# A streaming encoder layer on one core: three blocks of rows with eight products in place of the seven of the Strassen scheme

## Chip, core and metric

The kernel runs on one core of a Trainium2 chip. The metric is the device time of one execution in microseconds (us). The engines are TensorE (PE, with its weight loads as PEld), VectorE (DVE), ScalarE (ACT), GpSimd (POOL) and SyncE (SP, which here only issues transfers). Each works through its own queue in order.

## What is computed

One layer for 4096 prompt rows and 32 sample rows of width 1024. The rows are normalised, go through one input projection and two groups of heads, and the two halves go through an output projection:

```python
h = rms_norm(x, g_pre) * (1 + scale[:, None]) + shift[:, None]
proj = h @ w_in
z, xbc, dt_raw, u, v, gt = jnp.split(proj, [i1, i2, i3, i4, i5], axis=-1)
xbc, conv_new = causal_conv(xbc, conv_prev, conv_w, conv_b)
...
y, ssm_new = ssd_scan(xs, dt, a, bm, cm, ssm_prev)      # scan over chunks of 64 rows
ssd_out = (y + d_skip * xs) * jax.nn.silu(z)
v_n = layer_norm(v, g_v, beta_v)
gmlp_out = jax.nn.silu(gt) * u * gmlp_spatial(v_n, w_s, b_s)
mix = jnp.concatenate([ssd_out, gmlp_out], axis=-1) @ w_out
out = x + gate[:, None] * rms_norm(mix, g_post)
```

All of it is float32. `w_in` is 1024 x 5648, `w_out` 2048 x 1024.

## The kernel before

Weights and rows are split into a high and a low float16 half, and each product is the sum of three float16 matmuls (`PARTS`). The prompt is worked in eight blocks of 512 rows; the sample rows run along with block 3. A block goes: `super_step(0)` (B and C of the scan), the products for dt, the output projection of the block before it (16 weight tiles), `v_stage` (v, 14 tiles), and `super_step(1)` to `super_step(8)`. Each of the nine steps makes two pairs of 128-column strips, x and z, or gate and u. Work between them (conv, scan, spatial gating, row preparation of the next block) is put off with `later(lag, fn)` and called at a `tick` in a step, and a scheduler then lays out each engine's queue.

A step is a 2 x 2 block product with the seven products of the Strassen scheme in Winograd's form. `STEPS` lists them, each with 256 of the rows' columns: 7 x 2 x 12 = 168 matmuls. Sums of rows are made once a block in `phase_a_split` (L254 on VectorE, slots 4 to 6 of the rows' region); regions R0 and R1 alternate between blocks. Sums of weights are made once, in block 0: `stage_load` brings four strips of `w_in` (`stg`), `stage_squares` (L327, ScalarE) and `stage_scale` find a power of two for each and scale it (L341 on VectorE, or on ScalarE), and `wtile` makes a tile of each product:

```python
src = operand(s, w0[:, 0:512], w0[:, 512:1024], w1[:, 0:512], w1[:, 512:1024], ...)   # sums on VectorE, L302 to L308
split(wt[:, pi, 0], wt[:, pi, 1], src, nc.gpsimd if pi else nc.vector)                 # hi: ScalarE L266, lo: L267
nc.gpsimd.dma_start(out=w_dram[k][s], in_=...)                                         # L357, kept for the later blocks
```

`v_tile` does the same for v (tiles `wm`, sums `vtmp`, strips `vw`). Later blocks read the tiles back over SP's queue (L347 for `wt<-wd`, L409 for `wm<-vd`). Four slots hold weight tiles, and `wfetch(4)` asks for tiles up to four ahead. Results leave PSUM through `leave` (`LEAVES`): L661 on ScalarE where a quarter begins, L659 on VectorE where a product is added to it.

In block 1 the tiles of the output projection are made too: `o_tile` loads `wf`, and `split_w` makes hi (L295) and lo (L296) on VectorE.

Of the kernel before, what the change touches and what calls it, by code (L numbers as in the profile page):

```python
# [18 lines left out]
P = 128  # L19
# [34 lines left out]
PARTS = ((0, 0), (0, 1), (1, 0))  # L54

# [15 lines left out]
def hybrid_step_kernel(ctx: ExitStack, tc: tile.TileContext, io: dict, out: list):  # L71
# [143 lines left out]
    def new_rows(st, b):  # L215

        if st is prompt:
            st.hN = region(b, "hTp")
        else:
            st.hN = wk.tile([P, 3, 2, 4, st.T], F16, tag="hTs", name="hTs", bufs=1)  # L220
# [15 lines left out]
    def phase_a_split(st, ps, u, q, alt=False):  # L236
# [24 lines left out]
        for i, (src, slots, cs) in enumerate(parts):  # L261
            split(hN[:, slots, 0, q, cs], hN[:, slots, 1, q, cs], src, nc.vector if alt and i else nc.gpsimd)
# [17 lines left out]
    w_dram = [[dram.tile([P, 2048], F16, name=f"wd{k}_{s}", tag=f"wd{k}_{s}") for s in range(7)] for k in range(NSS)]  # L280
    v_dram = [dram.tile([P, 2048], F16, name=f"vd{j}", tag=f"vd{j}") for j in range(14)]
# [16 lines left out]
    def operand(s, a11, a12, a21, a22, tmp):  # L298

        tt = nc.vector.tensor_tensor  # L300
        if s == 1:
            tt(tmp, a21, a22, op=ALU.add)  # L302
        elif s == 2:
            tt(tmp, tmp, a11, op=ALU.subtract)
        elif s == 4:
            tt(a21, a11, a21, op=ALU.subtract)
        elif s == 5:
            tt(tmp, a12, tmp, op=ALU.subtract)  # L308
        return (a11, tmp, tmp, a12, a21, tmp, a22)[s]

# [3 lines left out]
    def stage_load(k):  # L314

        w = stage[k] = Work()
        w.f = [slots[(4 * k + n) % 8] for n in range(4)]
        for pi, (kind, i) in enumerate(SUPER[k]):
            for j in range(2):
                off = OFFS[kind][j] + i * P  # L320
                nc.sync.dma_start(out=w.f[2 * pi + j].rearrange("p (k c) -> p k c", c=P), in_=w_in_v[:, :, off:off + P])

    def stage_squares(k):
        w = stage[k]
        w.ss = small([P, 4], "wsq")
        for n in range(4):
            nc.scalar.activation(tmp2(prompt, "junk").bitcast(BF16), w.f[n], AF.Square, accum_out=w.ss[:, n:n + 1])  # L327

    def stage_scale(k):
        w = stage[k]  # L330
        s, inv = small([P, 4], "wsc"), scw[:, 4 * k:4 * k + 4]
        pow2_of_ssq(ssq_total(w.ss), [P, 4], "wp4", s, inv)
# [4 lines left out]
        for n in range(4):  # L337
            if n % 2:
                nc.scalar.activation(w.f[n], w.f[n], AF.Identity, scale=s[:, n:n + 1])
            else:  # L340
                nc.vector.tensor_scalar(w.f[n], w.f[n], s[:, n:n + 1], None, op0=ALU.mult)  # L341

    def wtile(k, s, first):
# [5 lines left out]
        w = stage[k]  # L349
        if s == 1:  # L350
            w.tmp = big("wtmp")
# [6 lines left out]
        return wt  # L358

# [32 lines left out]
    def mtile(d, idx, parts, s, first):  # L392
# [10 lines left out]
    vtmp = []  # L403

    def v_tile(s, h, first):
# [5 lines left out]
        if not vscale[0].known:  # L411
            for half in range(2):
                vscale[half].total()
                nc.vector.tensor_mul(sc_v[:, half:half + 1], vscale[half].inv, a_inv)
        if s == 0:
            for k in (2 * h, 2 * h + 1, 2 * h + 4, 2 * h + 5):
                nc.scalar.activation(vw[0][k], vw[0][k], AF.Identity, scale=vscale[0].s)
                nc.vector.tensor_scalar(vw[1][k], vw[1][k], vscale[1].s, None, op0=ALU.mult)
        if s == 1 and not vtmp:
            vtmp.extend(wk.tile([P, 512], F32, tag=tag, name="vtmp", bufs=n) for tag, n in (("xdtp", 1), ("xsTp", 3), ("xsTp", 3), ("xsTp", 3)))  # L420
        for qq in range(2):
            q = 2 * h + qq
            src = operand(s, vw[0][q], vw[0][q + 4], vw[1][q], vw[1][q + 4],
                          vtmp[2 * h + qq] if s else None)
            split(wt[:, qq, 0], wt[:, qq, 1], src, nc.gpsimd if qq else nc.vector)
# [15 lines left out]
    def plan():  # L441
# [6 lines left out]
        for b in range(NB):  # L448
            first = b == 0
            order.extend((wtile, (0, s, first)) for s in range(7))  # L450
            if b > 0:
                out(b == 1, 16)
            order.extend((v_tile, (s if first else STEPS_V[s][3], h, first)) for s in range(7) for h in range(2))
            order.extend((wtile, (k, s, first)) for k in range(1, NSS) for s in range(7))
# [210 lines left out]

    def super_step(k, active):
# [59 lines left out]
    def dt_rows_of(st, c):  # L726
# [115 lines left out]
    def by_rows(ps, x, w, first, last):  # L842
# [29 lines left out]
    def v_stage(active, first):  # L872
# [691 lines left out]
```

## Time and profile before

| | |
|---|---|
| median of 3 runs | 3115.49 us (3107.41 to 3121.79) |
| profiled execution, its time | 3119.56 us |
| profiled execution, span of the core | 3117.8 us |
| busy in the span | PE 2818.6, PEld 2016.7, DVE 1831.1, ACT 1499.6, POOL 1230.6 us |
| mean granted TensorE clock | 0.959 |
| DMA | 565.99 MB, 182 GB/s |

The span is the time from the first to the last instruction of the core, of one execution. A busy share over the whole span mixes block 0, in which weights are made, with blocks that only read them. The stretches used below are 0 to 104 us (opening and step 0 of block 0), 104 to 514 (the rest of block 0), 514 to 670 (block 1 to the end of its output projection), 670 to 893 (v and steps 1 to 8 of block 1) and 893 to 1240 (the same cycle of block 2 as a whole). The granted clock is the share of full speed (2.4 GHz) that TensorE was allowed; 0.5 is its lower level of 1.2 GHz.

### The profile page before, as it was taken

Reading aid. Unit: us, or ns where it says so; the run is one execution under the profiler, and the core shown is the slowest. Engines: PE = TensorE matmul, PEld = TensorE weight load, DVE = VectorE, ACT = ScalarE, POOL = GpSimd, SP = SyncE. Lnnn points to the kernel's source line nnn. Section 1 sums busy time; section 2 is a strip of 40 time slices with the busy share of each in tenths; the row PEclk is TensorE's granted clock in tenths of the full one; section 3 lists DMA queues with packets and bytes.
Section 4 is the critical chain, followed back from the end, with each engine's and each line's share of the span. In section 5 each row is a group of like instructions: output and inputs, shape, how many; then the busy total and the mean of one; then the engine's idle time right before and its main releaser. Section 6 shows DMA issues by size and latency. Waiting matters only on the chain. (4 is left out here: it accounts for less than half of the span.)

```text
span 3117.8 us, 56775 instructions
## 1 busy us (share of the span) xinstructions
PE 2818.6 (90%) x22010; PEld 2016.7 (65%) x22010; DVE 1831.1 (59%) x3938; ACT 1499.6 (48%) x3308; POOL 1230.6 (39%) x1143
## 2 busy tenths in 40 slices
PE   6766675789999999998999999999999999999988
PEld 2455564338874688546885478845885488747863
DVE  5987887956564554726557355545547455625562
ACT  4776764424544354534555335444545355424531
POOL 3556664323532254223553235432553144303441
PEclk7888888999999999999999999999999999999999
DMA  7655534566663766345564466636664566546652
GB/s 254 215 176 200 196 139 153 177 223 205 203 198 100 237 203 214 114 170 170 178 190 135 140 214 200 211 97 238 202 207 137 192 191 201 194 163 197 203 164 61
DMA packets 231335, 565.99 MB, mean 182 GB/s; under 512 B 26266, under 2 KB 76674, under 8 KB 231064
## 3 DMA queue, kind: packets, MB, share of 16 engines
q1 hardware_dynamic: 211400, 495.09, 49.9%
q0 software_dynamic: 19664, 67.27, 5.7%
q8 instruction: 172, 2.82, 0.4%
q14 instruction: 99, 0.81, 0.1%
HBM read 494.06 MB, written 68.20 MB: 180 GB/s over the span
## 5 line engine op out<-in xcount | busy, mean ns | idle before, releaser
L683 PE MATMUL ps_proj<-hTp,wt 128*128 128x256 f16 x12096 | 1428.4, 277 | 54.5 <-DVE zs L659 14.0
L683 PEld LDWEIGHTS <-wt 128*128 128x128 f16 x12096 | 1195.8, 100 | 226.9 <-issue 51.2
L851 PE MATMUL ps_out<-wm,mix 128*128 128x512 f16 x2880 | 654.0, 384 | 34.1 <-DVE wm L295 17.6
L851 PEld LDWEIGHTS <-mix 128*128 128x128 f16 x2880 | 281.7, 99 | 367.5 <-issue 39.5
L888 PE MATMUL ps_v<-wm,hTp 128*128 128x512 f16 x1344 | 306.9, 387 | 30.3 <-DMA wm<-vd 23.3
L888 PEld LDWEIGHTS <-hTp 128*128 128x128 f16 x1344 | 133.0, 100 | 197.0 <-issue 44.1
L1005 ACT ACTIVATE L<-L,acp 128x128 f32<-128x128 f32 x512 | 165.8, 390 | 144.8 <-DMA L<-acdp 132.3
L970 ACT ACTIVATE sq<-mix 128x512 f32<-128x512 f32 (+1 forms) x135 | 77.9, 582 | 306.8 <-POOL mix L1096 254.8
L723 DVE SCALAR_TENSOR_TENSOR xsT<-xp,cols,xsT 128x512 f32<-128x512 f32 (+1 forms) x216 | 223.0, 1035 | 3.7
L1068 DVE SCALAR_TENSOR_TENSOR hc<-hc,dcp,ps_s 128x64 f32<-128x64 f32 x384 | 79.9, 274 | 229.2 <-PE ps_s L1046 229.0
L1095 POOL TENSOR_TENSOR mix<-mix,E 128x512 f32<-128x512 f32 x72 | 84.1, 1167 | 305.5 <-DVE E L1091 296.7
L1016 POOL TENSOR_TENSOR L<-L,cb 128x512 f32<-128x512 f32 (+1 forms) x144 | 168.0, 1175 | 92.7 <-ACT L L1010 86.5
L267 POOL TENSOR_TENSOR mix<-ms,mix 128x512 f16<-128x512 f32 (+1 forms) x72 | 92.7, 1290 | 240.4 <-ACT mix L266 240.4
L974 POOL TENSOR_TENSOR acc<-acc,sq 128x512 f32<-128x512 f32 (+1 forms) x126 | 146.0, 1161 | 40.6 <-ACT sq L970 40.2
L267 POOL TENSOR_TENSOR hTp<-ta,hTp 128x512 f16<-128x512 f32 x64 | 78.1, 1221 | 199.4 <-ACT hTp L266 199.4
L267 POOL TENSOR_TENSOR v<-vt,v 128x512 f16<-128x512 f32 (+1 forms) x66 | 83.2, 1290 | 183.0 <-ACT v L266 183.0
L1102 POOL TENSOR_TENSOR mix<-mix,us 128x512 f32<-128x512 f32 x64 | 84.0, 1312 | 154.3 <-ACT us L661 142.7
L1038 POOL TENSOR_TENSOR xde<-xdt,dep 128x512 f32<-128x512 f32 x64 | 68.3, 1067 | 157.1 <-DVE xdt L1038 157.1
L254 DVE TENSOR_TENSOR tb<-ta 128x128 f32<-128x128 f32 x64 | 24.1, 376 | 171.2 <-ACT ta L245 166.2
L266 ACT ACTIVATE mix<-ms 128x512 f16<-128x512 f32 (+1 forms) x144 | 82.6, 582 | 83.1 <-DVE ms L1160 81.8
L1160 DVE TENSOR_TENSOR ms<-mix,sb 128x512 f32<-128x512 f32 (+1 forms) x144 | 108.5, 768 | 13.4 <-POOL hTp L267 8.9
L245 ACT ACTIVATE ta<-ps_xT,scol,gcol 128x256 f32<-128x256 f32 (+1 forms) x128 | 62.9, 543 | 104.4 <-PE ps_xT L232 90.3
(385 smaller groups left out, 4357.4 us busy)
## 6 DMA issues: line engine op xcount, KB each, us to landing
wt<-wd SPq DMA_DIRECT2D x441, 512.0 KB, 3.8
wm<-od SPq DMA_DIRECT2D x104, 512.0 KB, 3.5
wm<-vd SPq DMA_DIRECT2D x98, 512.0 KB, 5.1
L<-acdp SPq DMA_DIRECT2D x128, 256.0 KB, 4.4
wd<-wt POOLq DMA_DIRECT2D x63, 512.0 KB, 3.7
stg<-in_w_in_dram SPq DMA_DIRECT2D x36, 512.0 KB, 5.2
xa<-in_x_prompt_dram SPq DMA_DIRECT2D x32, 512.0 KB, 6.7
E<-acdp SPq DMA_DIRECT2D x128, 128.0 KB, 4.6
```

Of the source, the lines that this page charges most:

```text
L266: nc.scalar.activation(hi, src, AF.Copy)
L267: eng.tensor_tensor(lo, src, hi, op=ALU.subtract)
L683: nc.tensor.matmul(ps, wt[:, pi, a, q * P:(q + 1) * P], prompt.h[:, slot, b, q, :], start=(starts and h == 0 and n == 0), stop=(n == 11), ...
L723: nc.vector.scalar_tensor_tensor(dst, xp[:, k:k + Ts], w(k), dst, op0=ALU.mult, op1=ALU.add)
L851: nc.tensor.matmul(ps[c], x[kk][:, a, c * P:(c + 1) * P], w[:, kk, b, :], start=(first and n == 0), stop=(last and n == 5))
L888: nc.tensor.matmul(ps, prompt.h[:, slot, a, q, i * P:(i + 1) * P], wt[q // 2][:, q % 2, b, :], start=(starts and n == 0), stop=(n == 11), ...
L974: eng.tensor_tensor(st.accb if last else st.acc, st.acc, sq, op=ALU.add)
L1005: nc.scalar.activation(L[:, c, :], L[:, c, :], AF.Relu, scale=-1.0, bias=st.ac[:, c, 2 * j + hh:2 * j + hh + 1])
L1016: nc.gpsimd.tensor_tensor(w.L[hh], w.L[hh], st.cb[j // 4][0:st.Q], op=ALU.mult)
L1095: nc.gpsimd.tensor_tensor(w.m, w.m, w.E, op=ALU.add)
L1102: nc.gpsimd.tensor_tensor(m, m, w.d[1], op=ALU.mult)
L1160: nc.vector.tensor_tensor(t, m, sb, op=ALU.mult)
```

## The change

Blocks 0 to 2 (`b < FROM`) use `plain_step` and `v_plain`: eight products of 512 rows' columns, 96 matmuls a step and 192 for v, with the four plain tiles `PLAIN`, and results that leave PSUM 512 wide on ScalarE. Their rows fill only slots 0 to 3. The tiles of weight sums (`SUMS`), which blocks 3 to 7 need, are made by 22 jobs in the unused slots 4 to 6 of the rows' region (`spare`): ten are called in block 1, twelve in block 2. A job loads two pieces of 512 KB, scales them, makes four sums, splits each and stores four pieces of 256 KB. Beside that `o_tile` makes hi on ScalarE, staged strips are loaded and squared in halves two steps ahead, the last of them in spare room, and the preparation of block 1's rows is called in step 7 in place of step 8.

```diff
+FROM = 3
+PLAIN = (0, 3, 7, 6)
+SUMS = (1, 4, 2, 5)
...
+        elif st.plN:
+            parts = [(t.rearrange("p (i t) -> p i t", i=4), slice(0, 4), slice(u * P, (u + 1) * P))]
...
+    def spare(rows):
+
+        return rows[:, 4:7].rearrange("p i a k t -> p (i a k t)").bitcast(F32)
...
-        for n in range(4):
-            if n % 2:
-                nc.scalar.activation(w.f[n], w.f[n], AF.Identity, scale=s[:, n:n + 1])
-            else:
-                nc.vector.tensor_scalar(w.f[n], w.f[n], s[:, n:n + 1], None, op0=ALU.mult)
...
         for pi in range(2):
-            w0, w1 = w.f[2 * pi:2 * pi + 2]
-            src = operand(s, w0[:, 0:512], w0[:, 512:1024], w1[:, 0:512], w1[:, 512:1024],
-                          w.tmp[:, pi * 512:(pi + 1) * 512] if s else None)
-            split(wt[:, pi, 0], wt[:, pi, 1], src, nc.gpsimd if pi else nc.vector)
+            n = 2 * pi + j
+            scaled_split(wt[:, pi, 0], wt[:, pi, 1], stage[k].f[n][kh], sw[:, 4 * k + n:4 * k + n + 1], pi)
...
+    def scaled_split(hi, lo, wf, s, way):
+
+        if way == 0:
+            split_w(hi, lo, wf, s)
+        else:
+            nc.vector.tensor_scalar(wf, wf, s, None, op0=ALU.mult)
+            split(hi, lo, wf, nc.gpsimd)
...
+    def sums_load(kind, k, i):
+
+        w = Work()
+        f = spare(prompt.h)
+        w.a, w.b, w.t, w.o = f[:, 0:1024], f[:, 1024:2048], f[:, 2048:2560], f[:, 2560:3072]
...
+                nc.sync.dma_start(out=dst.rearrange("p (k c) -> p k c", c=P), in_=w_in_v[:, :, off:off + P])
...
+        later(5, sums_scale, w)
+
+    def sums_scale(w):
+        nc.scalar.activation(w.a, w.a, AF.Identity, scale=w.s[0])
+        nc.vector.tensor_scalar(w.b, w.b, w.s[1], None, op0=ALU.mult)
+        later(1, sums_first, w)
+
+    def sums_first(w):
+        a11, a21, a22 = w.a[:, 0:512], w.b[:, 0:512], w.b[:, 512:1024]
+        nc.vector.tensor_tensor(w.t, a21, a22, op=ALU.add)
+        nc.vector.tensor_tensor(a21, a11, a21, op=ALU.subtract)
+        later(1, sums_split, w, 1, w.t, w.o)
+        later(2, sums_split, w, 4, a21, a22)
+        later(2, sums_second, w, a11, a21)
...
+    def sums_split(w, s, src, out):
+
+        o = out.bitcast(F16)
+        split(o[:, 0:512], o[:, 512:1024], src, nc.gpsimd)
+        nc.gpsimd.dma_start(out=w.dst[s], in_=o)
...
         for hi, lo, wf in parts(wt):
-            split_w(hi, lo, wf, s)
+            nc.scalar.activation(hi, wf, AF.Identity, scale=s)
+            nc.vector.scalar_tensor_tensor(lo, wf, s, hi, op0=ALU.mult, op1=ALU.subtract)
...
+    def plain_step(k):
...
+        for j in range(2):
+            ps = [psum("ps_proj") for _ in range(2)]
+            for kh in range(2):
+                wt = wget()
...
+                        for a, b in PARTS:
+                            nc.tensor.matmul(ps[pi].rearrange("p (h t) -> p h t", h=2), wt[:, pi, a, q * P:(q + 1) * P],
+                                             prompt.h[:, 2 * kh:2 * kh + 2, b, q, :],
+                                             start=(kh == 0 and n == 0), stop=(kh == 1 and n == 11))
...
+                        nc.scalar.activation(ws[pi].d[j], ps[pi], AF.Identity, scale=scw[:, c:c + 1])
...
-                later((1 if b == 1 else 8) + (3 if b == 1 else 6) * q, phase_a_kt, prompt, xt, u, q)
+                later((1 if b == 1 else 8) + (2 if b == 1 else 6) * q, phase_a_kt, prompt, xt, u, q)
...
+        if b == 2:
+            for n, job in enumerate(jobs[10:]):
+                later(4 + 16 * n, sums_load, *job)
+        one_step(0)
...
+        if b == 1:
+            for n, job in enumerate(jobs[:10]):
+                later(4 + 16 * n, sums_load, *job)
+        v_stage(active, prompt.pl)
...
-            if first and b + 1 < NB and k == 8:
-                for u in range(2):
-                    later(6 + 13 * u, start_rows, b + 1, u, 1)
-            super_step(k, active)
+            if first and k + 2 < NSS:
+                later(2, stage_load, k + 2)
+                later(9, stage_squares, k + 2)
+                later(13, stage_scale, k + 2)
+            if first and k == 7:
+                later(2, start_rows, b + 1, 0, 1)
+                later(16, start_rows, b + 1, 1, 1)
+            one_step(k)
```

Three places of the queues show where the scheduler puts this. First VectorE in block 0, while the weights of a middle step are made. Before, its rows there are sums of staged strips (`wtmp<-...`, `stg<-stg`, L304 and L306) and the low halves of their splits (L267), with the moments of v (L919, L920) between:

```order
L267 TENSOR_TENSOR wt<-wtmp,wt 128x512
L919 BN_STATS bnp<-v 128x6
L304 TENSOR_TENSOR wtmp<-wtmp,stg 128x512
L920 BN_AGGR mvp<-bnp 128x2
L304 TENSOR_TENSOR wtmp<-wtmp,stg 128x512
L306 TENSOR_TENSOR stg<-stg 128x512
L267 TENSOR_TENSOR wt<-wtmp,wt 128x512
L306 TENSOR_TENSOR stg_247<-stg,stg_247 128x512
L267 TENSOR_TENSOR wt<-stg,wt 128x512
```

After, the hi (L303) and lo (L304) of one half tile stand between rows of the chunk work (conv L799 and L802, `xdt`, and the scan's results), with no sum among them:

```order
L303 TENSOR_SCALAR wt<-stg,sw 128x512
L1055 TENSOR_SCALAR vt<-v,mvp,nrp 128x512
L304 SCALAR_TENSOR_TENSOR wt<-stg,sw,wt 128x512
L1055 TENSOR_SCALAR vt<-v,mvp,nrp 128x512
L1190 SCALAR_TENSOR_TENSOR mix<-xsT,cols,ps_y 128x512
L1191 TENSOR_TENSOR E<-ps_o,E 128x512
L1157 COPY hc<-Hp 128x128
L303 TENSOR_SCALAR wt<-stg,sw 128x512
L1138 TENSOR_TENSOR xdt<-ps_xt,dtp 128x512
L304 SCALAR_TENSOR_TENSOR wt<-stg,sw,wt 128x512
L799 TENSOR_SCALAR xsT<-xp,cols 128x512
```

The sums have left this queue, and two short rows with one wait each took the place of a chain of sums in which each needs the one before.

Second SP's queue in block 1 near its steps 3 and 4: before, weight tiles (`wt<-wd`), rows of decay (`L<-acdp`) and one load of the spatial weights (`sp`):

```order
L347 DMA wt<-wd_0_108 128x2048
L347 DMA wt<-wd_1_109 128x2048
L995 DMA L<-acdp 128x512 x2
L347 DMA wt<-wd_2_110 128x2048
L347 DMA wt<-wd_3_111 128x2048
L615 DMA sp<-sp_dram 128x256
L347 DMA wt<-wd_4_112 128x2048
L347 DMA wt<-wd_5_113 128x2048
```

After, in the same steps, the loads of three jobs (L386, `hTp` is the rows' region with its spare slots) stand between the weight tiles (L353):

```order
L353 DMA wt<-wd_0_112 128x2048
L386 DMA hTp<-in_w_in_dram 128x8x128 x2
L353 DMA wt<-wd_3_115 128x2048
L353 DMA wt<-wd_7_119 128x2048
L1095 DMA L<-acdp 128x512 x2
L386 DMA hTp<-in_w_in_dram 128x8x128 x2
L353 DMA wt<-wd_6_118 128x2048
L669 DMA sp<-sp_dram 128x256
L1096 DMA E<-acdp 64x512 x2
L1095 DMA L<-acdp 128x512 x2
L353 DMA wt<-wd_0_120 128x2048
L386 DMA hTp<-in_w_in_dram 128x8x128 x2
```

A step has four tiles instead of seven, and behind each pair of job loads stand the next tiles that TensorE needs. All 22 jobs lie in the queues before step 6 of block 1, also the twelve that the code calls in block 2.

Third ScalarE in step 2 of block 1, after the change: a job's scaling (L396) and its copies to hi (L273) between results of the step (L741), decay rows (L1105) and activations:

```order
L396 ACTIVATE hTp<-hTp,sw 128x1024
L273 ACTIVATE hTp<-hTp 128x512 x4
L1070 ACTIVATE sq<-mix 128x512
L741 ACTIVATE zs<-ps_proj,scw 128x512
L1105 ACTIVATE L<-L,acp 128x128
L789 ACTIVATE zs<-zs 128x512
L1105 ACTIVATE L<-L,acp 128x128 x7
L741 ACTIVATE us<-ps_proj,scw 128x512
L1110 ACT_TABLE_LOAD
L1110 ACTIVATE L<-L 128x512 x2
L273 ACTIVATE hTp<-hTp 128x512
L396 ACTIVATE hTp<-hTp,sw 128x1024
```

Two scalings (L396) lie less than half a step apart here, and from three quarters of step 1 to two thirds of step 5 there are seven of them that use R0's spare slots.

## Rows read from the trace of the kernel before

**Rows 1.** Stretches of the span: busy us (instructions) of each engine, clock, DMA
```profile
core 0: us, PE busy (x) PEld busy (x) DVE busy (x) ACT busy (x) POOL busy (x), PEclk, DMA share, GB/s
104.00:514.00 410.00, 280.93 (x1994) 212.60 (x1993) 343.60 (x549) 282.13 (x576) 244.05 (x231) 0.84 0.54 185
514.00:670.00 156.00, 125.23 (x708) 64.77 (x707) 122.82 (x221) 57.90 (x115) 50.03 (x50) 0.95 0.51 164
670.00:893.00 223.00, 215.02 (x1858) 174.61 (x1857) 124.26 (x256) 104.33 (x238) 91.74 (x76) 1.00 0.68 218
893.00:1240.00 347.00, 337.50 (x2669) 247.35 (x2668) 188.52 (x424) 166.94 (x370) 134.08 (x116) 1.00 0.57 186
```

**Rows 2.** TensorE's waits, 104 to 514 us: total us, times, longest
```profile
PE ps_xT L232 <- DVE xa L212: 28.3, 2, 19.9
PE ps_xt L1023 <- ACT xsT L710: 25.7, 6, 6.4
```

**Rows 3.** Bare streams: `ps_proj` alone (1890 to 1990), then `ps_out` alone (900 to 1030)
```profile
1890.00:1990.00 100.00, 82.30 (x728) 13.49 (x28) 15.60 (x35) 1.00 0.63 200
...
900.00:1030.00 130.00, 85.33 (x384) 0.00 (x0) 0.00 (x0) 9.87 (x24) 1.00 0.45 153
```

**Rows 4.** By tile or line: stg, wtmp, vw, vtmp, L659, L661; tb twice; low halves
```profile
104.00:514.00 410.00, 138.69 (x112) 88.27 (x144) 39.25 (x32) 0.84 0.54 185
...
104.00:514.00 410.00, 89.54 (x72) 28.99 (x48) 30.57 (x24) 0.84 0.54 185
...
104.00:514.00 410.00, 15.61 (x24) 6.97 (x12) 10.12 (x7) 0.84 0.54 185
...
104.00:514.00 410.00, 13.56 (x18) 7.12 (x12) 8.42 (x6) 0.84 0.54 185
...
104.00:514.00 410.00, 27.78 (x56) 0.84 0.54 185
...
104.00:514.00 410.00, 33.91 (x74) 0.84 0.54 185
...
104.00:514.00 410.00, 9.00 (x16) 2.04 (x4) 3.74 (x4) 0.84 0.54 185
514.00:670.00 156.00, 12.64 (x32) 6.11 (x12) 13.87 (x12) 0.95 0.51 164
...
L267 DVE TENSOR_TENSOR wt<-wtmp,wt 128x512 f16<-128x512 f32 x24 | 20.6, 858 | 0.0
```

**Rows 5.** Groups, 104 to 514 us: busy us, mean ns | idle before
```profile
L295 DVE TENSOR_SCALAR wsT<-ws,gs_s 128x512 f16<-128x512 f32 x2 | 0.9, 474 | 0.0
...
L296 DVE SCALAR_TENSOR_TENSOR wsT<-ws,gs_s,wsT 128x512 f16<-128x512 f32 x2 | 1.4, 737 | 0.0
...
L341 DVE TENSOR_SCALAR stg<-stg,wsc 128x1024 f32<-128x1024 f32 x16 | 15.8, 1000 | 0.0
...
L302 DVE TENSOR_TENSOR wtmp<-stg 128x512 f32<-128x512 f32 x16 | 32.3, 2048 | 1.7 <-POOL wt L267 1.4
...
L302 DVE TENSOR_TENSOR vtmp<-vw 128x512 f32<-128x512 f32 x4 | 2.6, 679 | 0.0
...
L375 ACT ACTIVATE junk<-mix 128x512 bf16<-128x512 f32 x32 | 19.9, 622 | 14.6 <-DMA mix<-in_w_out_dram 14.1 <-POOL v L267 0.4
...
L375 ACT ACTIVATION_READ_ACCUMULATOR junk<-mix 128x1 f32 x32 | 6.1, 192 | 0.0
...
L661 ACT ACTIVATE v<-ps_v,sc_v 128x512 f32<-128x512 f32 x8 | 5.3, 675 | 2.3 <-PE ps_v L888 2.3
```

**Rows 6.** Groups, 514 to 670 us
```profile
L295 DVE TENSOR_SCALAR wm<-wf,go_s 128x1024 f16<-128x1024 f32 x16 | 13.3, 833 | 11.9 <-DMA wf<-in_w_out_dram 8.9 <-PE ps_out L851 3.0
```

**Rows 7.** Transfers (KB each, us to landing), and SP's waits, 670 to 893 us
```profile
wd<-wt POOLq DMA_DIRECT2D x63, 512.0 KB, 3.7
stg<-in_w_in_dram SPq DMA_DIRECT2D x36, 512.0 KB, 5.2
...
SPq L347 <- PE ps_proj L683: 109.7, 47, 4.5
```

More of the change, by code (lines that the diff above doesn't have):

```diff
@@ L261, in phase_a_split @@
         for i, (src, slots, cs) in enumerate(parts):
-            split(hN[:, slots, 0, q, cs], hN[:, slots, 1, q, cs], src, nc.vector if alt and i else nc.gpsimd)
+            split(hN[:, slots, 0, q, cs], hN[:, slots, 1, q, cs], src, nc.vector if alt else nc.gpsimd)
     def split(hi, lo, src, eng):
@@ L316, in stage_load @@
         w = stage[k] = Work()
[L317 to L321, printed above, removed]
+        if k < NSS - 1:
+            tiles = [slots[(4 * k + n) % 8] for n in range(4)]
+        else:
+            tiles = spare(prompt.h)
+            tiles = [tiles[:, n * DM:(n + 1) * DM] for n in range(3)]
+        w.f = [(t[:, 0:512], t[:, 512:1024]) for t in tiles]
+        if k == NSS - 1:
+            w.f.append([new_mix(prompt) for _ in range(2)])
+        for n in range(4):
+            kind, i = SUPER[k][n // 2]
+            off = OFFS[kind][n % 2] + i * P
+            for kh in range(2):
+                nc.sync.dma_start(out=w.f[n][kh].rearrange("p (k c) -> p k c", c=P),
+                                  in_=w_in_v[:, 4 * kh:4 * kh + 4, off:off + P])
+    def spare(rows):
+        return rows[:, 4:7].rearrange("p i a k t -> p (i a k t)").bitcast(F32)
     def stage_squares(k):
         w = stage[k]
[L325 removed]
+        w.ss = small([P, 2, 4], "wsq")
         for n in range(4):
[L327 removed]
+            for kh in range(2):
+                nc.scalar.activation(tmp2(prompt, "junk").bitcast(BF16)[:, 0:512], w.f[n][kh], AF.Square,
+                                     accum_out=w.ss[:, kh, n:n + 1])
     def stage_scale(k):
         w = stage[k]
[L331 to L332 removed]
+        s, inv = sw[:, 4 * k:4 * k + 4], scw[:, 4 * k:4 * k + 4]
+        nc.vector.tensor_tensor(w.ss[:, 0], w.ss[:, 0], w.ss[:, 1], op=ALU.add)
+        pow2_of_ssq(ssq_total(w.ss[:, 0]), [P, 4], "wp4", s, inv)
         if a_known:
@@ L410, in v_tile @@
             return wt
[L411 to L420, printed above, removed]
+        j, kh = divmod(PLAIN.index(s), 2)
+        if not vscale[j].known:
+            vscale[j].total()
+            nc.vector.tensor_mul(sc_v[:, j:j + 1], vscale[j].inv, a_inv)
         for qq in range(2):
[L422 to L425, printed above, removed]
+            scaled_split(wt[:, qq, 0], wt[:, qq, 1], vw[j][4 * kh + 2 * h + qq], vscale[j].s, qq)
         nc.gpsimd.dma_start(out=v_dram[2 * s + h], in_=wt.rearrange("p k a c -> p (k a c)"))
@@ L449, in plan @@
             first = b == 0
-            order.extend((wtile, (0, s, first)) for s in range(7))
+            seven = PLAIN if b < FROM else range(7)
+            order.extend((wtile, (0, s, first)) for s in seven)
             if b > 0:
                 out(b == 1, 16)
-            order.extend((v_tile, (s if first else STEPS_V[s][3], h, first)) for s in range(7) for h in range(2))
-            order.extend((wtile, (k, s, first)) for k in range(1, NSS) for s in range(7))
+            order.extend((v_tile, (s if b < FROM else STEPS_V[s][3], h, first)) for s in seven for h in range(2))
+            order.extend((wtile, (k, s, first)) for k in range(1, NSS) for s in seven)
         out(NB == 1, 16 if NB - 1 == SB else 8)
@@ L870, in by_token, with v_plain, rows_of, v_stage @@
             nc.tensor.transpose(ps[0:TS, ct * P:(ct + 1) * P], t[:, ct * TS:(ct + 1) * TS], ident)
-    def v_stage(active, first):
+    def v_plain():
+        for j in range(2):
+            ps = [psum("ps_v") for _ in range(NCH)]
+            for k2 in range(4):
+                wt = wget()
+                def rows_of(kk, a, c):
+                    return prompt.h[:, k2 // 2 * 2 + c // 2, a, k2 % 2 * 2 + kk, c % 2 * P:(c % 2 + 1) * P]
+                by_rows(ps, rows_of, wt, k2 == 0, k2 == 3)
+            for c in range(NCH):
+                nc.scalar.activation(prompt.v[c][:, j * 512:(j + 1) * 512], ps[c], AF.Identity, scale=sc_v[:, j:j + 1])
+    def v_stage(active, plain):
         for st in active:
             st.v = [big("v") for _ in range(st.nch)]
+        if plain:
+            v_plain()
+        else:
+            v_products(active)
+        for st in active:
+            mv = small([P, st.nch, 2], "mv" + st.name)
+            for c in range(st.nch):
+                later(1 + 2 * c, v_moments, st, c, mv)
+            later(1 + 2 * st.nch, v_norm, st, mv)
+    def v_products(active):
         acc = {}
@@ L878, in v_stage @@
             pv = ps_t.rearrange("p (a c t) -> p a c t", a=2, c=8)
-        steps = [(*x, s) for s, x in enumerate(STEPS)] if first else STEPS_V
-        for n_s, (name, starts, slot, s) in enumerate(steps):
+        for n_s, (name, starts, slot, s) in enumerate(STEPS_V):
             wt = [wget() for _ in range(2)]
```

93 lines of the change are left out of this document (57 added, 36 removed).

## The prediction

> **What bounds the kernel now.** I first cut the span at the places where the work changes: block 0 after the opening and its step 0, block 1 up to the end of its output projection, the rest of block 1, and one whole cycle of block 2 [rows 1]. In the last two rows TensorE is busy for 215 of 223 us and 338 of 347 us at a granted clock of 1.00: there the number and shape of matmuls set the time. The first row is another kernel: TensorE works 281 of 410 us at 0.84 of the clock, while VectorE is busy 344 us, 0.838 of the stretch, ScalarE 282 and GpSimd 244. Then the waits of that stretch [rows 2]: TensorE stands behind vector and scalar results that have nothing to do with its own tile (the transposes of block 1's rows, the chunk products). So block 0 is bound by the making of weights on three engines that work in order, VectorE first. In the second row VectorE is busy 123 of 156 us: the out tiles are made there.
>
> **The price of a plain product.** Two stretches give the rates of bare streams [rows 3]: 82.30 / 728 = 0.113 us for a 256-column matmul, 85.33 / 384 = 0.222 us for a 512-column one. A Strassen step is 168 x 0.113 = 19.0 us, a plain one 96 x 0.222 = 21.3: +2.3. The v products go from 168 to 192 matmuls of 512: +5.3. A whole block with nine steps costs 9 x 2.3 + 5.3 = **+26** where TensorE is the bound.
>
> The Trainium skill (TensorE: Matmul & The Clock Gate, "Back-to-back issue gap") has a rule that speaks for far more: in a sustained stream of weight loads and matmuls it gives some 131 ns for one of 512 columns. By it, as an estimate, a plain step takes 96 x 0.131 = 12.6 us against the row's 19.0 of a Strassen step, and with the v products a block gains about 55 us where it loses 26 by the rows, so that two blocks alone would bring the sum 162 us lower. The 384 matmuls of the row are such a stream, at 0.222 us: here the trace contradicts the page, and this outcome gets no chance.
>
> **Block 0 (104 to 514 us).** VectorE loses everything that touches the staged weights (138.7 us), the splits of summed tiles (20.6), the v sums (between 15.6 and 29.2; I take 21), the adding leaves (27.8: all leaves are plain and go to ScalarE) and the sums of rows (9.0) [rows 4]: 343.6 - 217.1 = 126.5. It gains 40 tiles (8 steps x 4, and 8 of v). A tile's first half is two operations of a kind whose rows say 0.474 and 0.737, its second half one scaling, half of 1.000 [rows 5]: 1.71 us, so 68 in all. The order puts about 4 of the 22 jobs at the end of block 0. A job is one scaling of 1024 and four sums of 512: 1.0 + 4 x 0.68 = 3.7 at the cheap price of a sum, 1.0 + 4 x 2.05 = 9.2 at the dear one; the same addition has both prices in these rows, dear where GpSimd splits beside it. VectorE ends at 210 to 232.
>
> ScalarE: 282.1 less staged and summed tiles (88.3, 29.0, 7.0, 7.1), less its 256-wide leaves (33.9 - 5.3), less 2.0 of rows is 120. It gains 40 copies of 0.622, 64 squares of halves of 0.622 + 0.192 and 32 wide leaves, which I price by the 0.675 of the eight wide ones of v (5.3 us for them) [rows 5]: 219, and with 4 jobs of 3.7 (two widths of 0.622, then four copies) 234. GpSimd: 244 less 39.3, 30.6, 10.1, 8.4 and 3.7 [rows 4], plus 40 splits of 30.57 / 24 = 1.27 and 4 jobs of four such is 223, with its transfers counted as before though they fall from 70 to 56. TensorE alone, at the pace of block 1, needs 223 + 8 x 2.3 + 5.3 = 247.
>
> No engine keeps the 344 of VectorE now; ScalarE's 234 at the present share of 0.838 gives 279 us. Three engines are then near their limit together where one is today, and TensorE at 247 would be as dense as in no stretch at 0.84 clock; I take 295, bounds 270 and 325: **-115** (-85 to -140). The opening loses eight sums and two scalings: **-8** (0 to -15, the sums between 0.68 and 2.05 each).
>
> **Block 1 up to the end of its out products.** VectorE's 122.8 loses the hi halves of the out tiles (13.3 [rows 6]; ScalarE, busy 58 of 156, takes them: hidden), the sums of rows (12.6 [rows 4]) and six leaves (6 x 0.5): 93.9. The order puts 7 jobs here. At 5 us each, between 3.7 and 9.2, VectorE has 129 us; at today's share of 122.8 / 156 = 0.787 that is 164 us: **+8**. If the jobs hide wholly, the freed hi halves give 5 back; at 9.2 us and some queueing behind them it is +45.
>
> **Block 1, v and steps 1 to 8.** The products cost 8 x 2.3 + 5.3 = +24. Into these steps the order packs eleven jobs, not into block 2. The seven that use region R0 have one work space, so one job's loads wait for the four stores of the job before. Those loads stand in SP's queue between the weight tiles of steps 1 to 5: whatever holds them holds the tiles behind. SP today waits for slots that TensorE frees, 109.7 us over 47 waits [rows 7], so four fetched tiles, one step's worth, are the cushion. A step takes (223 - 168 x 0.222) / 8 + 2.3 = 25.5 us. The scalings of R0's seven jobs lie in ScalarE's queue from 0.75 of step 1 to 0.65 of step 5: six intervals in 3.9 steps, 16.6 us for each. The chain of one job, bare: load 5.2, scaling 1.2, sum 0.7, copy 0.6, split 1.3, sum 0.7, copy 0.6, split 1.3, store 3.7 [rows 4, 5, 7], 15.3 us. It fits only with no queueing. If at each of the nine hand-overs about one leaf or half an operation lies ahead (0.75 us), a job takes 22; if an operation of the dear kind does (2.05), 33.8. I take 22, the shorter kind being by far the more frequent. The cushion swallows the first interval; five cost (22 - 16.6) x 5 = 27. Together **+51** (from the products alone, +24, to +90).
>
> **Block 2:** **+26** (24 to 28); no job is left in it. VectorE's sums of rows go, which TensorE hid (189 of 347 us busy); the leaves need 36 x 0.675 = 24 us of ScalarE where the eight narrow ones of each step needed 72 x (33.9 - 5.3) / 66 = 31, so they cost nothing even uncovered. Blocks 3 to 7 are unchanged.
>
> **Costed at nothing.** Staged loads come as eight transfers of 256 KB instead of four of 512, two steps ahead (some 50 us against 5.2 for the larger piece); if they were late, each step would begin up to 5 us late. Block 1's rows start a step earlier: four loads, four squares and the transposes, on an SP queue that in block 0 has only staged and chunk loads ahead of it. TensorE's wait for them is 28.3 us today [rows 2]; I leave what it may save inside the stretch's share. The jobs move 22 x 2 MB while plain steps read four tiles of 512 KB where seven were read, so the DMA share of block 1 (0.68) does not rise much.
>
> **Sum.** The profiled execution took 3119.6 us. 3119.6 - 8 - 115 + 8 + 51 + 26 = 3081.6. It ran 4.1 above the median of the runs, so against that median: **3078**. The upper ends of the two job terms belong to rivals B and C below; block 0's bound alone gives +30 upwards, and downwards the bounds of block 0, the out stage and the chain, as the root of their squares (25, 13, 27), give 39: 3040 to 3108.
>
> **Rivals.**
>
> A, the waits of block 0 go too. TensorE becomes the bound there with little idle time: 256 us instead of 295, the jobs' chains fit into the 16.6 us, and the out stage gains 5. For it: VectorE falls by a third and its queue stands ahead of most waits. Against: ScalarE and GpSimd were also over half busy, and lose less. 3119.6 - 8 - 154 - 5 + 24 + 26 - 4.1 = 2998.
>
> B, the dear price of sums holds in the new place. Jobs keep GpSimd splitting all through block 1's out stage, and each sum of a job reads two operands from SBUF; at 9.2 us a job the stage costs +50 instead of +8: 3120, no change. For it: 2.05 against 0.68 for the same addition. Against: the dear rows fall where VectorE and GpSimd worked on one tile.
>
> The Trainium skill (SBUF — State Buffer, "Who interferes with whom") says that a vector instruction with two inputs in SBUF contends with a GpSimd instruction that reads SBUF. By that rule case B is the likelier, the more jobs overlap; the two prices fit it, though no row separates it from other causes.
>
> C, the other side: SP's queue starves TensorE. Every microsecond of a job's chain above 16.6 costs five. From 33 us per job on the kernel is slower than today by over 0.5%; at 36 the sum is 3078 + 14 x 5 = 3148. The price is reached if hand-overs meet dear operations or if the stores wait on GpSimd's queue. For it: the in-order queues of four engines lie in one loop, and TensorE's tiles behind it. Against: block 1's VectorE and ScalarE are half idle (124 and 104 of 223 us).
>
> **How the numbers follow.** 0.5% either way (3100 to 3131) is about what a measurement of this kernel can tell from no change. My forecast gets 0.54, A 0.14, B 0.14, C 0.18. The forecast and A are faster: 0.68; B is the same: 0.14; C slower: 0.18. The range takes the forecast's own bounds, reaches to A below and to B and the beginning of C above: 2990 to 3130.
>
> **What will show it.** Right: the stretch of block 0 ends 85 to 140 us earlier, its granted clock rises, ScalarE and VectorE are about equally busy there; the rates of 0.222 hold and block 2 is 26 longer; in steps 1 to 5 of block 1 TensorE waits for tiles from the weight store some 27 us in all, with SP held by the jobs' stores. Wrong: jobs of over 30 us, sums of 2 us in the out stage, or a block 0 whose idle time stays because copies on ScalarE are now late.

## The result and the profile after

The changed kernel takes 3151.97 us (median of 4 runs, 3145.55 to 3156.24), the kernel before 3112.89 on the same chips: a ratio of 1.0121 (95% interval 1.0090 to 1.0152). It is slower by 1.2%, where 3078 us and faster was forecast, and above the upper end of the range.

Times below are medians of the executions at the usual granted clock; one execution, in the run with the low halves on VectorE and the jobs packed, fell to a clock of 0.748 and 3680.37 us and is left out.

The profiled execution spans 3154.5 us against 3117.8. Stretches of it, cut at the same products as before (first v product of block 0, first out product of blocks 1 and 2, first v product of block 1, first out product of block 3; same columns as [rows 1]):

```profile
84.00:430.00 346.00, 288.34 (x1539) 149.03 (x1537) 256.15 (x466) 243.16 (x520) 209.05 (x192) 0.92 0.60 190
430.00:578.00 148.00, 113.22 (x519) 50.57 (x518) 124.21 (x161) 77.97 (x125) 80.44 (x86) 0.86 0.68 223
578.00:923.00 345.00, 273.58 (x1443) 137.13 (x1442) 167.78 (x297) 162.17 (x293) 192.60 (x184) 0.92 0.57 185
923.00:1294.00 371.00, 357.99 (x2098) 190.95 (x2097) 158.79 (x362) 167.40 (x338) 132.37 (x113) 0.99 0.40 127
```

By the starts of these products (before, then after):

| stretch | before | after | change | forecast |
|---|---|---|---|---|
| opening, to v of block 0 | 103.8 | 83.9 | -19.9 | -8 |
| block 0 and block 1 to the end of its out products | 565.9 | 494.4 | -71.5 | -107 |
| v and steps of block 1, step 0 of block 2 | 245.5 | 344.9 | +99.5 | +53 |
| block 2's out, v, steps, step 0 of block 3 | 343.7 | 370.9 | +27.2 | +24 |
| the rest | 1858.9 | 1860.4 | +1.5 | 0 |

(The forecast's terms are divided at these places too: a plain step 0 of 2.3 us moves from block 2's term to the line above.) The largest miss is in the third row, 46 us beyond its forecast; the second row misses by 36. In the third row TensorE, at 1.00 of the clock before [rows 1], is busy 273.58 of 345 us at 0.92. Its waits there, and SP's (total us, times, longest):

```profile
PE ps_xt L1123 <- ACT xsT L789: 58.3, 6, 22.5
PE ps_proj L733 <- DMA wt<-wd: 11.0, 2, 8.0
```

```profile
SPq L386 <- DMA wd<-hTp: 115.2, 22, 15.9
SPq L353 <- PE ps_proj L733: 98.2, 21, 15.6
```

SP was held by the jobs' stores as foreseen, 115.2 us over 22 waits, but TensorE waited only 11.0 us for a weight tile, 8.0 of it before step 1. It waited 58.3 for the transposes of x, which come after a strip has left PSUM (L741), gone through the conv (L799, L802) and been activated (L789). The longest of these waits, from the time-ordered view of the changed kernel (start, duration, idle before):

```profile
628.94 12.56 PE L733 MATMUL ps_proj<-hTp,wt 128*128 128x512 f16 x48 [7.97 <-DMA wt<-wd]
...
643.31 0.76 DVE L397 TENSOR_SCALAR hTp<-hTp,sw 128x1024 f32<-128x1024 f32 x1 [5.29 <-DMA hTp<-in_w_in_dram]
...
644.53 4.06 PE L733 MATMUL ps_proj<-hTp,wt 128*128 128x512 f16 x18 [3.03 <-DMA wt<-wd]
...
645.29 0.63 ACT L273 ACTIVATE hTp<-hTp 128x512 f16<-128x512 f32 x1 [5.71 <-DVE hTp L402]
...
653.78 0.68 DVE L414 TENSOR_TENSOR hTp<-hTp 128x512 f32<-128x512 f32 x1
...
657.66 0.69 DVE L414 TENSOR_TENSOR hTp<-hTp 128x512 f32<-128x512 f32 x1
...
658.38 0.63 ACT L273 ACTIVATE hTp<-hTp 128x512 f16<-128x512 f32 x1 [3.25 <-DVE hTp L414]
...
661.43 0.67 ACT L741 ACTIVATE xp<-ps_proj,scw 128x512 f32<-128x512 f32 x1
...
670.40 0.63 ACT L789 ACTIVATE xsT<-xsT 128x512 f32<-128x512 f32 x1
...
671.08 1.11 PE L1123 MATMUL ps_xt<-ident,xsT 128*128 128x128 f32 x4 [22.49 <-ACT xsT L789]
```

The products of a step's first x strip are complete after 36 matmuls (`plain_step`), here at about 639; the next 30 matmuls are done at 648.6, and then the transposes of that strip stand ahead of all further products in TensorE's queue. ScalarE takes the strip only at 661.4: ahead of it stand copies of two jobs, which wait for a job's loads and for VectorE's sums, and work on v of the step itself. The conv and the activation end at 671.0.

The second row of the table has waits of the same kind. In the out products of block 1 (429.5 to 578.2) TensorE waits for both halves of the out tiles, low and high, which are made beside seven jobs:

```profile
PE ps_out L932 <- DVE wm L463: 18.6, 8, 4.1
PE ps_out L932 <- ACT wm L462: 16.2, 8, 6.3
```

Together this is 34.8 us, where the kernel before waits 20.8 for these tiles.

A job's pace was as forecast. The scalings of the seven jobs in R0, first and last, ScalarE in order of time:

```profile
679.34 1.14 ACT L396 ACTIVATE hTp<-hTp,sw 128x1024 f32<-128x1024 f32 x1
...
815.98 1.13 ACT L396 ACTIVATE hTp<-hTp,sw 128x1024 f32<-128x1024 f32 x1
```

Six intervals in 136.6 us are 22.8 us each; 22 was taken.

### The profile page after: what moved, and what is told of

It is laid out like the page before. It is cut to its first block, busy times and chain, and to the rows that moved or that the text cites. A ratio compares the mean times of both kernels' runs of the same rounds, so it can differ in the third digit from the quotient of the medians.

```text
span 3154.5 us, 52782 instructions
## 1 busy us (share of the span) xinstructions
PE 2866.3 (91%) x20090; PEld 1819.5 (58%) x20090; DVE 1734.6 (55%) x3706; ACT 1521.0 (48%) x3260; POOL 1309.0 (41%) x1229
## 5 line engine op out<-in xcount | busy, mean ns | idle before, releaser
L762 PE MATMUL ps_proj<-hTp,wt 128*128 128x256 f16 x7560 | 874.4, 274 | 13.5 <-DMA wt<-wd 6.1
L762 PEld LDWEIGHTS <-wt 128*128 128x128 f16 x7560 | 738.4, 98 | 105.0 <-issue 9.7
L932 PE MATMUL ps_out<-wm,mix 128*128 128x512 f16 x2880 | 660.8, 387 | 52.4 <-DVE wm L463 18.6
L733 PE MATMUL ps_proj<-hTp,wt 128*128 128x512 f16 x2592 | 602.4, 390 | 11.0 <-DMA wt<-wd 11.0
L733 PEld LDWEIGHTS <-wt 128*128 128x128 f16 x2592 | 257.9, 100 | 309.4 <-issue 29.9
L1105 ACT ACTIVATE L<-L,acp 128x128 f32<-128x128 f32 x512 | 166.5, 392 | 135.5 <-DMA L<-acdp 111.5
L802 DVE SCALAR_TENSOR_TENSOR xsT<-xp,cols,xsT 128x512 f32<-128x512 f32 (+1 forms) x216 | 226.2, 1049 | 4.5
L1116 POOL TENSOR_TENSOR L<-L,cb 128x512 f32<-128x512 f32 (+1 forms) x144 | 176.5, 1235 | 108.8 <-ACT L L1110 100.0
L993 PE MATMUL ps_v<-wm,hTp 128*128 128x512 f16 x840 | 188.2, 383 | 15.6 <-DMA wm<-vd 14.5
L993 PEld LDWEIGHTS <-hTp 128*128 128x128 f16 x840 | 82.6, 99 | 118.8 <-issue 23.2
L1123 PE MATMUL ps_xt<-ident,xsT 128*128 128x128 f32 (+1 forms) x264 | 47.3, 303 | 104.9 <-ACT xsT L789 104.9
L274 POOL TENSOR_TENSOR hTp<-hTp 128x512 f16<-128x512 f32 x88 | 107.4, 1225 | 69.9 <-ACT hTp L273 67.0
```

The source lines that it names most:

```text
L274: eng.tensor_tensor(lo, src, hi, op=ALU.subtract)
L733: nc.tensor.matmul(ps[pi].rearrange("p (h t) -> p h t", h=2), wt[:, pi, a, q * P:(q + 1) * P], prompt.h[:, 2 * kh:2 * kh + 2, b, q, :], st ...
L762: nc.tensor.matmul(ps, wt[:, pi, a, q * P:(q + 1) * P], prompt.h[:, slot, b, q, :], start=(starts and h == 0 and n == 0), stop=(n == 11), ...
L802: nc.vector.scalar_tensor_tensor(dst, xp[:, k:k + Ts], w(k), dst, op0=ALU.mult, op1=ALU.add)
L932: nc.tensor.matmul(ps[c], x(kk, a, c), w[:, kk, b, :], start=(first and n == 0), stop=(last and n == 5))
L993: nc.tensor.matmul(ps, prompt.h[:, slot, a, q, i * P:(i + 1) * P], wt[q // 2][:, q % 2, b, :], start=(starts and n == 0), stop=(n == 11), ...
```

## Experiments

Theories. **S**: SP, held by the jobs' loads, is late with weight tiles (the prediction's). **Q**: operations of jobs stand ahead of strip, conv and activation in the in-order queues, and TensorE's queue has the transposes of x too close behind. **K**: GpSimd's work beside VectorE's makes the latter longer. "The stretch" is the third row of the table from the first product of step 1 of block 1: 204 us before, 294.2 in the change. The kernel before took 3107 to 3109 us beside these runs and 3113 beside the change, so differences between times below are good to some 6 us.

**No jobs.** The kernel leaves out the sums of weights: both calls of `later(..., sums_load, *job)` are gone, and blocks 3 to 7 read a plain tile where they would read a sum, for v in the same way:

```diff
-            nc.sync.dma_start(out=wt.rearrange("p i a c -> p (i a c)"), in_=w_dram[k][s])
+            nc.sync.dma_start(out=wt.rearrange("p i a c -> p (i a c)"), in_=w_dram[k][(0, 0, 3, 3, 7, 7, 6, 7)[s]])
...
```

> The 22 jobs that make sums of weights are left out, and blocks 3 to 7 read a plain tile wherever they would read a sum (same size and order of transfers, so the output is not the reference's). Theory 1 (the jobs, packed into block 1, cost what was lost): the stretch from the first product of block 1's step 1 to block 2's output projection falls from 294 us to about 222 (the 204 of the kernel before and 8 x 2.3), the output projection of block 1 from 149 to 127 to 132, v by 4: about 3057 us, 3045 to 3070. Rival (the eight products themselves cost more beside the conv, scan and gating than their matmul rate says): over 3110 us.

Measured 3040.32 us, ratio 0.978 (0.977 to 0.980): the jobs cost some 112 us, 5.1 each, more than theory 1 gave them. Block 0 and block 1 to the end of its out products take 449.4 us, 45 less than with jobs. The stretch takes 241.5, not 222, and TensorE still waits for x, with no job there:

```profile
PE ps_xt L1123 <- ACT xsT L789: 16.1, 6, 5.0
```

**Jobs spread.** Each job's loads are queued behind the weight tile last called for (`last[0]` is set where `wtile`, `v_tile` and `mtile` load one); the work is the same:

```diff
...
+    def sums_load(*job):
+        with tc.issue_after(last[0].ins):
+            sums_load_now(*job)
...
```

> Same jobs, but each job's loads stand in SP's queue behind the weight tile that was last called for where the code calls the job: ten jobs in block 1, twelve in block 2, one in about 20 to 25 us. Theory 1 (too many jobs in too short a stretch, their operations placed earlier in the in-order queues than a job can deliver): the stretch of block 1 comes back to about 225 us, its output projection to about 130, block 2 gains 0 to 15: about 3070 us, 3060 to 3090. Rival (what counts is the work of the jobs, wherever it lies): 3140 to 3155 us.

Measured 3134.86 us (1.0085, 1.007 to 1.010): 17 us better, no more. The stretch still takes 287.5, and block 2 loses 44 us, about as much as block 0 and block 1's out products gain. That the jobs were packed together was a small part; a job costs over 4 us wherever it lies.

**Loads on GpSimd's queue.** In `sums_load`, `nc.sync.dma_start` becomes `nc.gpsimd.dma_start`.

> The changed kernel with the loads of the jobs issued by GpSimd's queue instead of SP's. Theory S (the step of the prediction: SP, held by the jobs' loads, is late with TensorE's weight tiles): about 3100 us, since the tiles are no longer behind the loads. Theory Q (the jobs' copies, scalings and sums stand ahead of the step's own work in the queues of ScalarE and VectorE, and TensorE waits for the transposes of x): within 15 us of 3152, TensorE's wait for xsT in that stretch still over 45 us.

Measured 3179.57 us (1.023). Weight tiles are no longer behind job loads and TensorE waits for none in the stretch, but the kernel is 28 us slower, and the wait for x is 83.3 us. GpSimd's own queue now stands behind the stores (23.7 us in block 1), so the 28 us are no price of S; but with no wait for a tile left and the loss still there, S has fallen as the main cause.

**Scaling and copies on GpSimd.**

```diff
-        nc.scalar.activation(w.a, w.a, AF.Identity, scale=w.s[0])
+        nc.gpsimd.tensor_scalar(w.a, w.a, w.s[0], None, op0=ALU.mult)
...
-        split(o[:, 0:512], o[:, 512:1024], src, nc.gpsimd)
+        nc.gpsimd.tensor_copy(o[:, 0:512], src)
+        nc.gpsimd.tensor_tensor(o[:, 512:1024], src, o[:, 0:512], op=ALU.subtract)
```

> The changed kernel with the jobs' scaling of one piece and their copies to the high half on GpSimd instead of ScalarE; loads and everything else as in the change. Theory Q (ScalarE's queue holds the results of the step and of x behind operations of the jobs): TensorE's wait for xsT falls from 58 us to under 25 and the time to 3110 to 3140 us, although a job takes longer. Theory S (only the length of a job's chain counts): a job is some 3 us longer, six intervals: 3165 to 3180 us.

Measured 3196.69 us (1.028), above both. ScalarE's queue alone was not it: TensorE waits 76.1 us for x. GpSimd's scaling took 2.94 us in the mean of steps 1 to 8 where ScalarE's takes 1.15, so a longer job and more work on GpSimd are both in this number.

**Transposes of x five ticks later** in blocks 0 to 2 (`st.pl`), once with the jobs spread and once in the change as it is:

```diff
-        lag = 7 if j == 1 else 0
+        lag = (7 if j == 1 else 0) + (5 if st.pl else 0)
```

> As the run with the jobs spread (3135 us), and in blocks 0 to 2 the decay and the transposes of x are called five ticks later after their strip (some 30 matmuls further down TensorE's queue). Theory Q (operations of the jobs delay strip, conv and activation of x, and TensorE's queue has the transposes right behind, so every delay stops it): the wait for xsT falls from 50 us to under 15 in block 1's steps, 3070 to 3090 us. Theory K (GpSimd's splits and VectorE's two-operand work hold each other up, and all of the step gets longer): 3125 to 3140 us.

> The changed kernel, jobs where the scheduler put them, with the transposes of x five ticks later as in the run beside it. Theory Q: the wait for xsT in block 1 falls from 58 us to under 25, and the time to 3095 to 3115 us; what is left are jobs that are later than a shift of 7 us. Theory K: within 15 us of 3152.

Measured 3089.48 (45 less than spread alone; 0.994, 0.992 to 0.996) and 3127.60 (24 less than the change). With the jobs spread the stretch falls from 287.5 to 254.1 us, as Q had it. With them packed the time is above what Q expected (3095 to 3115), as there are new waits beside what is left of the old one:

```profile
PE ps_s L1146 <- POOL xde L1138: 26.7, 6, 7.9
PE ps_xt L1123 <- ACT xsT L789: 18.7, 1, 18.7
```

**Jobs behind the conv.** `later(4 + 16 * n, ...)` becomes `later(9 + 16 * n, ...)`, on the spread kernel.

> As the run with the jobs spread, but each job is called five ticks later in its step (tick 9 of 16 in place of 4), so that its scaling, sums and splits stand behind the strip, the conv and the activation of x in the queues of ScalarE and VectorE instead of among them; the transposes stay where they were. Theory Q: a job then costs under 2 us instead of 4 to 5, the wait for xsT in block 1 is near the 16 us that it is without jobs: 3065 to 3090 us. Theory K: the same work beside the same engines, 3125 to 3140 us.

Measured 3112.91 us (1.001): 22 us, between the theories. The queues have the jobs behind x, and the wait for x is 32.1 us instead of 50.2. Order is not all.

**Low halves on VectorE**, spread and packed:

```diff
-        split(o[:, 0:512], o[:, 512:1024], src, nc.gpsimd)
+        split(o[:, 0:512], o[:, 512:1024], src, nc.vector)
```

> As the run with the jobs spread, with the low halves of the jobs made on VectorE instead of GpSimd. Theory K (GpSimd's splits hold up VectorE): the jobs' sums fall to 0.68 us each and the time to 3090 to 3115 us. Theory Q: four more operations of 0.7 to 0.9 us for each job stand before the conv in VectorE's queue, 3140 to 3160 us.

> The changed kernel with one edit: the low halves of the jobs on VectorE; jobs stay packed in block 1 and transposes where they were. If GpSimd's splits beside VectorE are a main part of the 112 us that the jobs cost, 3095 to 3115 us. If the packing alone decides, 3140 to 3175 us, since VectorE gets four more operations for each job in a stretch of which it is already a link.

Measured 3091.30 us (44 less than spread) and 3109.08 (43 less than the change; 1.000 to before): as K had it both times, although VectorE does four more operations a job. The conv of x in the stretch, spread kernel and then this edit (busy us, mean ns | idle before):

```profile
L808 DVE SCALAR_TENSOR_TENSOR xsT<-xp,cols,xsT 128x512 f32<-128x512 f32 x24 | 26.6, 1110 | 0.4
...
L805 DVE TENSOR_SCALAR xsT<-xp,cols 128x512 f32<-128x512 f32 x8 | 11.3, 1408 | 3.5 <-ACT xp L747 3.5
...
L415 DVE TENSOR_TENSOR hTp<-hTp 128x512 f32<-128x512 f32 x9 | 10.5, 1171 | 23.4 <-POOL hTp L274 23.4
```

```profile
L808 DVE SCALAR_TENSOR_TENSOR xsT<-xp,cols,xsT 128x512 f32<-128x512 f32 x24 | 19.5, 817 | 0.2
...
L415 DVE TENSOR_TENSOR hTp<-hTp 128x512 f32<-128x512 f32 x9 | 6.1, 680 | 0.0
...
L805 DVE TENSOR_SCALAR xsT<-xp,cols 128x512 f32<-128x512 f32 x8 | 4.8, 595 | 3.5 <-ACT xp L747 3.5
```

Two things went: a conv of 37.9 us became 24.3, and VectorE no longer waits for GpSimd before a sum (23.4 us at L415). But the conv is not dear by the jobs alone. Its second line in the stretch of the run without jobs, and of the kernel before:

```profile
L802 DVE SCALAR_TENSOR_TENSOR xsT<-xp,cols,xsT 128x512 f32<-128x512 f32 x24 | 26.9, 1121 | 0.8
```

```profile
L723 DVE SCALAR_TENSOR_TENSOR xsT<-xp,cols,xsT 128x512 f32<-128x512 f32 x24 | 28.0, 1168 | 0.5
```

The whole conv takes 33.0 us there without jobs, 32.8 before and 35.1 in the change. The jobs' sums show more of it. Two of a job's four in the stretch of the change, then L409 in block 1's out products:

```profile
L414 DVE TENSOR_TENSOR hTp<-hTp 128x512 f32<-128x512 f32 x10 | 8.8, 879 | 21.4 <-POOL hTp L274 21.4
L409 DVE TENSOR_TENSOR hTp<-hTp 128x512 f32<-128x512 f32 x10 | 8.5, 855 | 8.9 <-POOL hTp L274 8.9
```

```profile
L409 DVE TENSOR_TENSOR hTp<-hTp 128x512 f32<-128x512 f32 x7 | 11.9, 1700 | 0.0
```

In the stretch of the change VectorE mostly waits for GpSimd's splits, 30 us before these sums; in the out products it is slowed. There it is busy 124.9 us, and 115.7 with the low halves made on VectorE, though these add 17.3 us and only four sums fewer lie there.

The next two runs take the wait away and keep GpSimd busy. On the spread kernel with VectorE's low halves they give GpSimd as much work back, which nobody waits for, once reading (below, behind each store) and once only writing (four `nc.gpsimd.memset(idle16, 0.0)` in its place):

```diff
+        with tc.issue_after(ins.ins):
+            nc.gpsimd.tensor_tensor(idle16, ones.unsqueeze(1).to_broadcast([P, 4, P]),
+                                    tri.unsqueeze(1).to_broadcast([P, 4, P]), op=ALU.subtract)
```

> As the run with the jobs spread and their low halves on VectorE (3091 us), and after each of a job's four stores GpSimd does a subtraction of 512 columns on two constants, which nobody waits for (four operations of about 1.2 us for each job, as many as the splits that it no longer does). Theory L (GpSimd working in SBUF lengthens what VectorE does beside it): conv and sums are as long as with the splits on GpSimd again and the time returns most of the way to 3135 us: 3115 to 3140. Theory W (VectorE, in order, waited for GpSimd's splits before it could write the next sum, 33 us in block 1): nobody waits for these, so 3085 to 3105 us.

> As the run beside it, with four short fills of a constant (256 columns each, about 1.2 us together) after each store in place of the subtraction: GpSimd is as busy, but reads nothing. If reads are what collides, conv and sums keep their short times and the run stays at 3085 to 3105 us; if any work of GpSimd does it, it goes where the run beside it goes.

Measured 3146.83 us, above the range of theory L, and 3092.43. The stretch of each (columns as in [rows 1]), reading first:

```profile
578.00:862.00 284.00, 232.70 (x1250) 119.22 (x1251) 183.07 (x272) 145.81 (x252) 169.34 (x151) 0.93 0.52 173
```

```profile
574.00:838.00 264.00, 231.13 (x1251) 117.99 (x1250) 150.41 (x272) 145.09 (x253) 166.68 (x262) 0.94 0.54 181
```

The same 272 operations of VectorE take 183 us beside a GpSimd that reads for its 169, and 150 beside one that writes for its 167. TensorE waits 48.2 us for x in the one and 32.9 in the other. So GpSimd's reads cost, 54 us in this pair. What the in-order wait alone is worth is not shown: neither run has it, but in the reading run VectorE also makes the low halves beside the reads (38.8 us, and 30.3 beside the writes), which the spread kernel leaves to GpSimd.

**All together**, with and without the shift of the jobs in their step, and the transposes late with no jobs at all:

> Jobs spread and behind the conv, low halves of the jobs on VectorE, transposes of x five ticks later: the three edits that each gained alone, together. If the two causes (operations of jobs ahead of the chain that TensorE waits for; GpSimd's splits lengthening VectorE's work) are separate, the gains add up to 3135 - 22 - 45 - 44 = 3024 us, and cannot go below the run without jobs and with late transposes: 3020 to 3055 us. If they are one cause seen twice, the second edit finds little left: 3075 to 3090 us.

> As the run beside it without the shift of the jobs in their step: spread, low halves on VectorE, late transposes. Separate causes: 3135 - 44 - 45 = 3046 us, 3035 to 3065. One cause: 3075 to 3090 us.

> The jobs left out as in the run without jobs (blocks 3 to 7 read plain tiles for sums), and the transposes of x five ticks later. If the 16 us that TensorE waits for xsT in block 1 without any job come from the plain step itself (its x strip leaves late for the transposes that stand behind it), blocks 1 and 2 each lose about 15 us: 3010 us, 3000 to 3020. Otherwise 3035 to 3045 us.

Measured 3047.58 us (0.980, 0.978 to 0.982), 3062.15 (0.985, 0.983 to 0.988) and 3002.71 (0.966). The first two lie in the ranges for separate causes, the third in that for a wait which the plain step has of itself. Most of the gains add up: 87 us off the spread kernel where 111 would be the plain sum. The stretch without jobs, and with the three edits and all jobs:

```profile
575.00:795.00 220.00, 220.00 (x1251) 115.41 (x1250) 88.32 (x196) 116.26 (x206) 94.43 (x76) 1.00 0.39 130
```

```profile
578.00:811.00 233.00, 224.23 (x1252) 116.64 (x1250) 152.81 (x280) 137.00 (x248) 116.85 (x111) 0.99 0.61 203
```

TensorE is never idle in the first; in the second it is busy 224 of 233 us at 0.99 of the clock. The jobs now cost 45 us, 2.0 each, and the change with these edits gains 2% instead of losing 1.2%.

## Why the prediction was wrong

- **The step that failed: "Block 1, v and steps 1 to 8 ... +51".** With the step 0 that is counted here, 53 was forecast and 99.5 measured. The jobs are 62 of it (344.9 us against 282.9 without them), where 27 was forecast, and the products are 37.5, where 26 was (15.8 with the transposes late). The pace of a job was right (22.8 us against 22), and SP was held as described. What failed is the link from there to TensorE, "whatever holds them holds the tiles behind": TensorE waited 11.0 us for tiles. (Whether the cushion took the rest is not shown: the steps were 36.8 us long by then, 294.2 / 8, where 25.5 was taken, which left the jobs time.) The jobs' price came by the queues of ScalarE and VectorE, from which TensorE needs x soon after the strip: 58.3 us of waits at x, of which 16.1 stay without jobs, and a clock of 0.92 (0.98 without jobs), at which the 1443 matmuls of the row took 273.6 us instead of 266.9. I had rejected this with "block 1's VectorE and ScalarE are half idle". That is an average; the chain strip, conv, activation, transposes has some 30 matmuls (about 6.5 us) of slack in TensorE's queue, and a job puts several operations ahead of it.
- **Rival B had the mechanism, but not its size.** The dear price of VectorE's work beside a reading GpSimd (2.05 against 0.68 us, [rows 5]) holds also on tiles that the two do not share, which I had put against it: in the reading run GpSimd reads only constants. In the out products one of a job's four sums was dear (1700 ns), and the stage went from 132.4 to 148.7 us, +16 where B had +50 and my forecast +8. In the steps of block 1 the sums took 31.5 us, where 39 of the cheap kind are 26.5, and the conv 35.1 where 33.0: only some 7 us of the row's 62. The Trainium skill (SBUF — State Buffer, "Who interferes with whom") says that a two-input vector instruction contends with GpSimd instructions that read SBUF and not with those that only write. The reading and writing runs agree: 183 and 150 us. Rival C's time (3148) came true by another way than its own.
- **Block 0** lost 88 us with the jobs at its end (433.5 to 345.7, to block 1's first out product), just inside its bounds of 85 to 140. Without jobs, opening apart, it and block 1's out stage lose 116.5 us, where 115 and 5 were forecast. The jobs at its end and in the out stage cost 45 us. I had allowed 13 for the seven in the out stage, by their busy time on VectorE, which leaves out what waits behind them. The opening gained 19.9, more than twice the forecast and beyond its bound of 15; why is not shown.
- **+26 for a plain block** met +27.2, but partly by luck. In block 2, with no job in it, TensorE waits 12.2 us for x; with the transposes late and no jobs the same stretch is 355.2 us, +11.5. The 512-column rate of [rows 3] was a little high: in block 2 the changed kernel's v runs 192 matmuls in 41.60 us, 0.217 each. That contradicts again the 131 ns of the Trainium skill (TensorE: Matmul & The Clock Gate, "Back-to-back issue gap") and agrees with the about 216 ns that the same section gives for a single matmul.
- **Costed at nothing** and right, as far as the waits show: the reads of fewer tiles and the staged halves. The hi halves of the out tiles on ScalarE were not wholly hidden: TensorE waits 8.6 us for them without jobs and 16.2 beside them, though the out stage without jobs is 122.2 us against 132.4.

Not settled: how the 43 us of the low halves on GpSimd divide between VectorE's waits for the splits and its slower work beside them, what the remaining 45 us of the jobs are made of, and how much of the packed kernel's loss is in which of two overlapping jobs.

## What to carry to other kernels

Work put "beside" a busy TensorE is priced at the chain that TensorE waits for next, not at the mean load of the engines: find how many matmuls stand between a strip's last product and the first instruction that needs what VectorE and ScalarE make of it, and give background work that much slack or put it behind that chain. Before moving subtractions or copies to an idle GpSimd, ask what VectorE reads in the same microseconds and which of its operations wait for the result: here the "free" engine cost 43 us, and doing its work on VectorE was cheaper. A job that fits its pace can still cost its whole length if it is queued in order ahead of the critical work.

## What the runs showed of the hardware

VectorE's one-input operation of the conv (`TENSOR_SCALAR`, 128 x 512) took 1408 ns in the mean of the stretch with the jobs spread, 595 with their low halves on VectorE, and 734 and 630 in the reading and the writing run. So it too can be more than twice as long, but GpSimd's reads as such lengthen it little, and what did it in the first of these runs is open. GpSimd that filled memory for as long as it had read cost nothing measurable (3092.43 against 3091.30 us).
